# A hybrid attention block on one core: the attention's product with the values as fp32 matmuls of one query block, the mask inside the scan, and one 32-wide inverse by a transpose

## The chip, the cores and the metric

The kernel runs on one core of a Trainium2 chip. A core has five engines that run their own instruction queues side by side: PE (TensorE, matrix products, with its weight loads shown as a row of their own, PEld), DVE (VectorE), ACT (ScalarE), POOL (GpSimd) and SP (SyncE, which here only issues DMAs). The metric is the device time of one execution in microseconds (us). The kernel before takes 717.94 us (median of three runs, 717.68 to 718.83).

## The reference

The input is 1024 tokens of 1024 channels. After an RMS norm, one projection gives the inputs of two groups of heads that work side by side: eight heads of stick-breaking attention (64 channels each) and four heads of a gated DeltaNet (128 channels each). Both outputs are normed and gated, then one output projection, the residual and a last norm follow. What the change touches is the attention, and one step in the DeltaNet's triangular inverse:

```
z    = q_block @ k[:end].T / sqrt(64)            # one block of 128 queries, keys 0 .. end
causal = s < t
tail = sum over s < j < t of softplus(z[t, j])
attn = where(causal, exp(log_sigmoid(z) - tail), 0)
o    = attn @ v[:end]
```

The weight of key s for query t is thus sigmoid(z[t, s]) times the product of 1 - sigmoid(z[t, j]) over the keys j between s and t. Everything is float32.

## The kernel before, in words

All arithmetic is written through helper recorders, so nearly every instruction has the line 315 (the call in `Recorder`); instructions are told apart by the names of their tiles. The order of the work is set by a planner inside the kernel (`Model`, `Stream`, `interleave`). Each part of the program is a generator (`attention`, `window`, `delta_solve`, `delta_scan`, `projections` and so on) that emits instructions and yields a condition or a result to wait for. The planner keeps a clock of its own with a cost for every instruction (`cost`, and in `pull` a least distance between the starts of two matmuls), takes the ready generator of the lowest priority number, and so fixes the order on each engine before anything runs. The projections have the number 100 and fill PE where no attention (10) and no DeltaNet (0 to 0.7) is ready. On the chip each engine then works through its list in that order.

Stages. First the query projections, then the values and the keys of the first heads, then a long middle in which attention, DeltaNet and the remaining projections are interleaved, and last the output projection. A product in "high and low" form splits a float32 operand into a part rounded to fp32r (a float32 format whose matmul shows as one record in the trace) and the rest, and adds the products (`mm3` uses three; the names end in h and l).

Attention runs over eight heads, and in each over four windows of two query blocks (`window`, `w` from 0 to 3; a token for each window, and at most three at once). For each block of 128 queries:

- PE makes z in a PSUM bank (`pz`) from `q2` and the keys in high and low form, `kh` and `kl`. On the last 128 keys, the diagonal block, a third matmul (`maskr` by `ident`) adds -1e30 where the key isn't before the query.
- ACT writes sigmoid(z) to `sg` and sigmoid(-z) back to the bank. DVE runs a scan from the last key to the first (`cc`, the running product). POOL multiplies `sg` by `cc` shifted by one key: the attention weights, queries on partitions, keys along the row.
- PE transposes them 128 by 128 (`ident`, `sg`) into `pz`, up to four blocks at a time. ACT copies these to `ah` (fp32r) and DVE puts the rest into `al`.
- PE multiplies with the values. The stationary operand is `v2a`, 128 keys by 128 columns: 64 of the values' high part and 64 of their low part (`v2e`, written by `v_evac` with one ACT and one DVE instruction). The moving operand is `ah`, then `al`, for both query blocks at once (256 columns). The sum is in the one bank `po`, values on partitions.
- ACT copies it to `o`, PE transposes it back (`ident`, `o`), DVE adds the high and the low half (`oe`), SP stores it.

In the DeltaNet's inverse (`gdn_inv`), 32 by 32 blocks are inverted from 16 by 16 ones. Both the inverse (`xc`) and its transpose (`wc`) are updated by 16 small matmuls each (`xc`, `yt` and `yt`, `xc`), and DVE adds both results.

Of the kernel before, what the change touches and what calls it, by code (L numbers as in the profile page):

```python
# [29 lines left out]
WINDOWS = 3  # L30
# [107 lines left out]
class Model:  # L138
# [141 lines left out]
    def pull(self):  # L280
        if self.pe and not self.pe_busy and not self.pe[0].waits:
# [3 lines left out]
            at = max(self.now, op.ready, self.pe_began + 0.834 * op.columns)  # L285
# [137 lines left out]
def block(tc, xT_d, x_d, n1_d, wE_d, wQ_d, wC_d, conv_d, alog_d, dtb_d, mixw_d, wo_d, fnw_d, out_d):  # L423
# [4 lines left out]
    with ExitStack() as top:  # L428
# [34 lines left out]
        maskr = cst.tile([P, P], F32R, name="maskr")  # L463
        rbc = cst.tile([P, T], F32, name="rbc")
        make_identity(nc, rbc[:, 0:P])
        A.activation(identr, rbc[:, 0:P], AF.Copy)
# [5 lines left out]
        v_s = dr.tile([NB, P, SBH, 2, SBD], F32R, name="v_s")  # L472
# [57 lines left out]
        for tag, bufs in (("kh", 1), ("kl", 1), ("q2", 1), ("v2a", 2), ("v2a", 2), ("cc", 2), ("cc", 2), ("sg3", 1)):  # L530
            chl.append(at_.tile([P, 2, 520], F32R, tag=tag, bufs=bufs, name="chl"))
        sm = at_.tile([P, 768], F32, tag="sg2", name="sm")
# [63 lines left out]
        def diagonal(g):  # L596
            dg = at_.tile([P, 2, P], F32, tag="o2", bufs=2, name="dg")
# [18 lines left out]

        G.affine_select(zero, zero, pattern=[[-1, P]], compare_op=ALU.is_gt, fill=-1e30, base=0, channel_multiplier=1)
        A.activation(maskr, zero, AF.Copy)
# [12 lines left out]
        busy = {"w0": 0, "w1": 0, "w2": 0, "w3": 0, "T": 0, "al": 0, "po": 0, "inv": 0}  # L631
# [3 lines left out]
        def values(part):  # L635
            cs = slice(264 * part, 264 + 256 * part)
            n = 264 - 8 * part
            for b in range(NB):
                if part == 0 and 4 < b < 7:
                    row_scale(b - 5, dgs)  # L640
                if part == 0 and 4 <= b < 6:
                    dgs = [diagonal(2 * (b - 4) + g) for g in range(2)]
# [16 lines left out]
        def decays(me):  # L659
# [35 lines left out]
            cs = at_.tile([P, 2 * P], F32, tag="al", bufs=2, name="cs")  # L695
# [247 lines left out]
        def gdn_inv(h, g):  # L943
# [39 lines left out]
            xv = x0p[:, 0:2 * P].rearrange("p (u c i) -> p u c i", u=2, c=4)  # L983
# [121 lines left out]
        def attention():  # L1105
            yield lambda: "sp" in flags
            for i in range(2):
                ccs.append(at_.tile([P, T + 1], F32, tag="cc", bufs=2, name="cc"))
                V.memset(ccs[i][:, T:T + 1], 1.0)
            for h in range(SBH):  # L1110
                yield lambda: f"k{h // 2}" in flags
                kh = at_.tile([P, T], F32R, tag="kh", name="kh")
                kl = at_.tile([P, T], F32R, tag="kl", name="kl")
                q2 = at_.tile([P, T], F32R, tag="q2", name="q2")
                v2 = at_.tile([P, NB, P], F32R, tag="v2a", bufs=2, name="v2a")
# [6 lines left out]
                S.dma_start(v2.bitcast(F32), v_s[:, :, h].rearrange("b s u d -> s b (u d)").bitcast(F32))  # L1122
                hd[h] = (q2, kh, kl, v2)
# [288 lines left out]
```

## Time and profile before

| what | value |
|---|---|
| median of 3 runs | 717.94 us |
| the profiled execution | 717.07 us, its span 715.3 us |
| PE busy | 692.1 us, 97% of the span |
| DVE busy | 554.8 us, 78% |
| ACT busy | 364.6 us, 51% |
| POOL busy | 262.1 us, 37% |
| mean granted PE clock | 0.989 |
| DMA, share of 16 engines | 41% |

The span runs from the first to the last instruction; 1.8 us of the execution lie around it. Matmuls overlap one another, and each is drawn with a modelled end, so PE's busy time overstates what it does: what a matmul takes of PE is read from the distance between two starts. A float32 matmul that isn't in fp32r shows as two records, with two weight loads. In a row of a timeline, the first number is the start and the second the length, both in us, then engine, line, operation and tiles, `x` how many were merged into the row, and in brackets how long the engine had been idle and what ended it.

### The profile page before, as it was taken

How to read it: one execution, taken by the hardware profiler on the slowest of the kernel's cores; microseconds unless marked ns; L12 is line 12 of the kernel's file. 1: busy time of each engine (PE TensorE's matmuls, PEld its weight loads, DVE VectorE, ACT ScalarE, POOL GpSimd, SP SyncE). 2: the span in 40 equal slices, each digit the busy share in tenths (PEclk: the TensorE clock that was granted, in tenths of full speed). 3: DMA queues.
4: the chain of work that ended last, by engine and by line, in shares of the span. 5: the costliest groups of instructions: out<-in, count | busy, mean ns of one | idle time of the engine just before them, and what ended most of it. 6: DMA issues, size and time to landing. Idle time of an engine off the chain costs nothing.

```text
span 715.3 us, 13641 instructions
## 1 busy us (share of the span) xinstructions
PE 692.1 (97%) x4830; PEld 585.8 (82%) x4830; DVE 554.8 (78%) x1463; ACT 364.6 (51%) x887; POOL 262.1 (37%) x224
## 2 busy tenths in 40 slices
PE   8999999999899999999999899999999999899995
PEld 7889998888778888778888789888879888678885
DVE  5463616669899998968899778989788887898843
ACT  5661247437657542435667446866467852421212
POOL 0000157535434324232443244554244474443221
PEclk9999999999999999999999899999999999999998
DMA  8945374280512042226225027341615275646321
GB/s 313 359 144 213 118 269 148 71 254 7 177 38 61 24 122 65 63 75 211 60 65 155 29 78 214 101 157 45 192 58 168 61 228 191 226 163 211 100 100 59
DMA packets 76500, 96.45 MB, mean 135 GB/s; under 512 B 24656, under 2 KB 45712, under 8 KB 76432
## 3 DMA queue, kind: packets, MB, share of 16 engines
q1 hardware_dynamic: 76432, 95.58, 41.1%
q8 instruction: 38, 0.62, 0.4%
q14 instruction: 30, 0.25, 0.1%
HBM read 67.67 MB, written 27.89 MB: 134 GB/s over the span
## 4 chain that ended last, share of the span: by engine, by line
PE 78%; DVE 16%; issue 3%; ACT 2%; POOL 1%; POOLq 0%; DVEq 0%
PE pp L315 49%; PE pz L315 21%; PE po L315 6%; PE pc L315 3%; DVE cc L315 2%; DVE tm L315 2%; DVE pp L315 2%; DVE al L315 1%; DVE ac L315 1%; DVE xs L315 1%; DVE w L315 1%; DVE y L315 1%; DVE xinv L315 1%; DVE pre L315 1%; DVE wol L315 1%
## 5 line engine op out<-in xcount | busy, mean ns | idle before, releaser
L315 PE MATMUL pp<-xh,weh 128*128 128x512 f32 x384 | 162.4, 423 | 0.4 <-DVE ac L315 0.2
L315 PE MATMUL pp<-xh,wel 128*128 128x512 f32 x384 | 151.5, 394 | 0.0
L315 PE MATMUL pp<-xl,weh 128*128 128x512 f32 x384 | 150.9, 393 | 0.0
L315 POOL TENSOR_TENSOR sg<-sg,cc 128x128 f32<-128x128 f32 (+3 forms) x64 | 77.0, 1206 | 104.2 <-DVE cc L315 51.2
L315 POOL TENSOR_TENSOR wel<-wer,weh 128x512 fp32r<-128x512 f32 x48 | 61.9, 1292 | 97.8 <-ACT weh L315 86.7
L315 PEld LDWEIGHTS pp<-xh,wel 128*128 128x128 f32 x384 | 72.5, 189 | 16.2
L315 PEld LDWEIGHTS pp<-xh,weh 128*128 128x128 f32 x384 | 72.9, 190 | 12.0 <-issue 0.9
L315 PEld LDWEIGHTS pp<-xl,weh 128*128 128x128 f32 x384 | 73.0, 190 | 9.7
L315 ACT ACTIVATE sg<-pz,rs 128x384 f32<-128x384 f32 (+3 forms) x96 | 54.0, 588 | 23.7 <-PE pz L315 22.9
L315 ACT ACTIVATE ah<-pz 128x512 fp32r<-128x512 f32 (+1 forms) x80 | 43.5, 560 | 33.9 <-PE pz L315 33.2
L315 DVE TENSOR_TENSOR_SCAN cc<-pz,one 128x384 f32<-128x384 f32 (+2 forms) x64 | 54.0, 848 | 3.5 <-ACT pz L315 3.1
L315 DVE TENSOR_TENSOR al<-pz,ah 128x512 fp32r<-128x512 f32 (+1 forms) x80 | 49.9, 630 | 6.5 <-ACT ah L315 5.9
L315 PE MATMUL pp<-wol,mh 128*128 128x512 f32 (+1 forms) x136 | 52.0, 383 | 1.1 <-DVE wol L315 1.1
L315 PE MATMUL pp<-woh,mh 128*128 128x512 f32 (+1 forms) x136 | 52.4, 385 | 0.0
L315 ACT ACTIVATE pz<-pz,ns 128x384 f32<-128x384 f32 (+3 forms) x96 | 52.1, 566 | 0.0
L315 PE MATMUL pp<-woh,ml 128*128 128x512 f32 (+1 forms) x136 | 51.8, 381 | 0.0
L315 DVE TENSOR_TENSOR tm<-xs,br 128x8 f32<-128x8 f32 (+14 forms) x120 | 49.9, 416 | 0.8
L315 PE MATMUL pp<-chl,xh 128*128 128x264 f32 (+1 forms) x256 | 46.8, 284 | 0.0
L315 PE MATMUL pz<-ident,sg 128*128 128x128 f32 x288 | 43.7, 277 | 3.0 <-DVE cc L315 1.4
L315 PE MATMUL po<-ah,v2a 128*128 128x256 f32 (+1 forms) x160 | 43.5, 295 | 0.0
L315 DVE SCALAR_TENSOR_TENSOR pp<-pre,conv,pp 128x512 f32<-128x512 f32 x48 | 36.1, 752 | 7.8 <-ACT pp L315 7.5
L315 DVE TENSOR_TENSOR_SCAN cc<-pz,cc,one 128x512 f32<-128x512 f32 (+1 forms) x32 | 38.7, 1210 | 1.9 <-ACT pz L315 1.5
(240 smaller groups left out, 1649.6 us busy)
## 6 DMA issues: line engine op xcount, KB each, us to landing
wer<-wE SPq DMA_DIRECT2D x48, 256.0 KB, 3.8
xr<-x SPq DMA_DIRECT2D x16, 512.0 KB, 6.5
qk_s<-xq SPq DMA_DIRECT2D x8, 512.0 KB, 5.1
v_s<-v2e SPq DMA_DIRECT2D x16, 256.0 KB, 2.0
q<-qk_s SPq DMA_DIRECT2D x8, 512.0 KB, 4.5
v2a<-v_s SPq DMA_DIRECT2D x8, 512.0 KB, 7.3
kh<-qk_s SPq DMA_DIRECT2D x8, 512.0 KB, 4.0
kl<-qk_s SPq DMA_DIRECT2D x8, 512.0 KB, 6.0
```

The source lines that it names most:

```text
L315: ins = f(*args, **kw).ins
```

## The change

The product with the values. The attention weights are transposed as before, but ACT copies them into one float32 tile `at`, and nothing is split. `at` is now the stationary operand, 128 keys by 128 queries, and the values are the moving one, 64 columns of plain float32 (`va`). The result has queries on partitions, so it is copied by ACT (`oe`) and stored as it is: the transpose back, the copy `o` and the DVE sum are gone. The values are written by one ACT copy each (`ve`), at half the size. Work goes by single query blocks: eight windows for a head, a token for each, at most six at once.

The mask. The -1e30 matmul is gone. A tile `step` holds 384 columns of zeros and then the identity; the scan reads it backwards on the diagonal block, starts from 0, and takes max(z' * state, step) in place of a product: on the diagonal the state becomes 1, and nothing before it counts. Elsewhere it takes the maximum with 0.

The 32-wide inverse. The transpose `wc` is updated by its 16 matmuls, and `xc` is made from it by a DVE transpose; the other 16 matmuls and one DVE addition are gone.

The planner's least distance between two matmul starts goes by the type of the stationary operand's matmul (0.42 ns a column for fp32r, 0.834 for float32), and a few tiles have other buffers. The kernel's numbers (`WINDOWS`) and tile tags aside, this is the diff:

```diff
-WINDOWS = 3
+WINDOWS = 6
...
-            op.columns = int(np.prod(inputs[0].shape[1:]))
+            op.load = int(np.prod(inputs[0].shape[1:])) * (0.42 if inputs[0].dtype == F32R else 0.834)
...
-            at = max(self.now, op.ready, self.pe_began + 0.834 * op.columns)
+            at = max(self.now, op.ready, self.pe_began + op.load)
...
-        identr = cst.tile([P, P], F32R, name="ident")
-        ident = identr.bitcast(F32)
-        one = cst.tile([P, 1], F32, name="one")
-        V.memset(one, 1.0)
+        step = cst.tile([P, 512], F32, name="step")
+        ident = step[:, 384:512]
...
-            v2 = at_.tile([P, 4, 2, SBD], F32R, tag=("al", "ah")[b % 2], bufs=2, name="v2e")
-            A.activation(v2[:, :, 0, :], src, AF.Copy, scale=rstd[:, b:b + 1])
-            V.scalar_tensor_tensor(v2[:, :, 1, :], src, rstd[:, b:b + 1], v2[:, :, 0, :].bitcast(F32), ALU.mult, ALU.subtract)
-            S.dma_start(v_s[b, :, h0:h0 + 4, :, :].bitcast(F32), v2.bitcast(F32))
+            ve = at_.tile([P, 4, SBD], F32, tag="at", bufs=3, name="ve")
+            A.activation(ve, src, AF.Copy, scale=rstd[:, b:b + 1])
+            S.dma_start(v_s[b, :, h0:h0 + 4, :], ve)
...
-                    TE.matmul(xv[quads[q], 1, c, :], xc[quads[q], c, :], yt[quads[q], c, :], start=True, stop=True)
-            for q in range(4):
-                if q == 0:
-                    yield
-                for c in range(4):
-                    TE.matmul(xv[quads[q], 0, c, :], yt[quads[q], c, :], xc[quads[q], c, :], start=True, stop=True)
-            r = [V.tensor_tensor(wc, xv[:, 1], wc, ALU.add), V.tensor_tensor(xc, xv[:, 0], xc, ALU.add)]
+                    TE.matmul(xv[quads[q], c, :], xc[quads[q], c, :], yt[quads[q], c, :], start=True, stop=True)
+            V.tensor_tensor(wc, xv, wc, ALU.add)
+            r = V.transpose(xc.rearrange("p c i -> p (c i)"), wc.rearrange("p c i -> p (c i)"))
...
-                    if s1 == end:
-                        TE.matmul(z[:, n - P:n], identr, maskr, start=False, stop=False)
...
-                    V.tensor_tensor_scan(cc[:, s0:s1][:, ::-1], z[:, 0:n][:, ::-1], one.to_broadcast([P, n]),
-                                         1.0 if s1 == end else cc[:, s1:s1 + 1], ALU.mult, ALU.mult)
+                own = step[:, 512 - n:512][:, ::-1] if s1 == end else step[:, 0:1].to_broadcast([P, n])
+                V.tensor_tensor_scan(cc[:, s0:s1][:, ::-1], z[:, 0:n][:, ::-1], own,
+                                     0.0 if s1 == end else cc[:, s1:s1 + 1], ALU.mult, ALU.max)
...
-                    ah = at_.tile([P, 512], F32R, tag="ah", bufs=2, name="ah")
-                    al = at_.tile([P, 512], F32R, tag="al", bufs=2, name="al")
-                    A.activation(ah[:, 0:n * P], tp[:, 0:n * P], AF.Copy)
-                    r = V.tensor_tensor(al[:, 0:n * P], tp[:, 0:n * P], ah[:, 0:n * P].bitcast(F32), ALU.subtract)
+                    at = at_.tile([P, 512], F32, tag="at", bufs=3, name="at")
+                    r = A.activation(at[:, 0:n * P], tp[:, 0:n * P], AF.Copy)
...
-                    for m, t in enumerate((ah, al)):
-                        TE.matmul(ov[:, i0 * P:256], v2[:, s, :], t[:, c], start=(s == 0 and m == 0), stop=(s == 2 * w + 1 and m == 1))
+                for u in range(n):
+                    k = 4 * (j - 1) + u
+                    TE.matmul(ov, at[:, u * P:(u + 1) * P], va[:, k, :], start=k == 0, stop=k == b)
...
-            o2 = at_.tile([P, 256], F32, tag="o2", bufs=2, name="o2")
-            yield A.activation(o2, ov[:, 0:256], AF.Copy)
+            oe = at_.tile([P, SBD], F32, tag="oe", bufs=4, name="oe")
+            yield A.activation(oe, ov, AF.Copy)
             busy["po"] = 0
-            op = pz()
-            for i in range(2):
-                TE.transpose(op[:, i * P:(i + 1) * P], o2[:, i * P:(i + 1) * P], ident)
-            oe = at_.tile([P, 2, SBD], F32, tag="oe", bufs=2, name="oe")
-            V.tensor_reduce(oe, op[:, 0:256].rearrange("p (i u d) -> p i d u", i=2, u=2), AX.X, ALU.add)
-            flags[f"e{h}{w}"] = S.dma_start(o_s[2 * w:2 * w + 2, :, h * SBD:(h + 1) * SBD].rearrange("b t d -> t b d"), oe)
+            flags[f"e{h}{b}"] = S.dma_start(o_s[b, :, h * SBD:(h + 1) * SBD], oe)
```

How the order moves, at two places. On PE, in the last window of the first head, before the change (`o` and `sg` are transposed, `ident` is the identity; numbers behind a name tell one buffer from another):

```order
L315 MATMUL po<-ah,v2a 128x256
L315 MATMUL po<-al,v2a 128x256
L315 MATMUL po<-ah,v2a 128x128
L315 MATMUL po<-al,v2a 128x128
L315 MATMUL pz<-kh,q_1537 128x512
L315 MATMUL pz<-maskr,ident 128x128
L315 MATMUL pz<-kl,q_1537 128x512
L315 MATMUL pz<-kh,q_1537 128x512
L315 MATMUL pz<-kl,q_1537 128x512
L315 MATMUL pz<-ident,o_2046 128x128 x2
L315 MATMUL pz<-ident,sg 128x128 x8
```

On PE at the same place after the change, from the first head's query block 5 to 7 (`step` now holds the identity):

```order
L315 MATMUL pz<-kh,q_1512 128x512
L315 MATMUL pz<-kl,q_1512 128x512
L315 MATMUL po<-va,at 128x64 x6
L315 MATMUL pz<-step,sg 128x128 x7
L315 MATMUL po<-va,at 128x64 x7
L315 MATMUL pp<-xh,weh 128x512
L315 MATMUL pp<-xl,weh 128x512
L315 MATMUL pp<-xh,wel 128x512
```

The mask matmuls and the transposes of `o` are gone, and a block's products stand together, as many as it has key blocks, where groups of `ah` and `al` stood; the transposes of `sg` and the pairs of `kh` and `kl` stay. Between two groups of products there are other matmuls, but at one place here only the next transposes.

On DVE at that place before the change (`tm` and `xs` are the DeltaNet's 16-wide inverse, `pre` a projection's result, the `cc` rows are the scans):

```order
L315 TENSOR_TENSOR al<-pz,ah 128x512
L315 TENSOR_TENSOR tm<-xs,br 128x64
L315 TENSOR_TENSOR al<-pz,ah 128x512
L315 TENSOR_REDUCE xs<-tm 128x4
L315 SCALAR_TENSOR_TENSOR cc<-pz,one 128x512
L315 TENSOR_TENSOR al<-pz,ah 128x384
L315 SCALAR_TENSOR_TENSOR cc<-pz,cc,one 128x512
L315 COPY pre<-pre 128x3
L315 TENSOR_TENSOR pre<-pp,rbc 128x512
L315 TENSOR_REDUCE oe<-pz 128x128
```

And on DVE after the change, between the scans of the first head's last blocks:

```order
L315 SCALAR_TENSOR_TENSOR cc<-pz,step 128x384
L315 TENSOR_TENSOR tm<-xs,br 128x4x11
L315 SCALAR_TENSOR_TENSOR cc<-pz,cc,step 128x512
L315 TENSOR_REDUCE xs<-tm 128x4
L315 MEMSET pre 128x3
L315 TENSOR_TENSOR pre<-pp,rbc 128x512
L315 TENSOR_TENSOR tm<-xs,br 128x4x12
L315 SCALAR_TENSOR_TENSOR pp<-pre,conv,pp 128x512
```

Of the attention only the scans are left on DVE; `al` and `oe` no longer stand between them and the rest.

More of the change, by code (lines that the diff above doesn't have):

```diff
@@ L462, in block @@
         ns8 = cst.tile([P, NB], F32, name="ns8")
-        maskr = cst.tile([P, P], F32R, name="maskr")
         rbc = cst.tile([P, T], F32, name="rbc")
-        make_identity(nc, rbc[:, 0:P])
-        A.activation(identr, rbc[:, 0:P], AF.Copy)
+        make_identity(nc, ident)
+        V.memset(step[:, 0:384], 0.0)
         rsg = cst.tile([P, GH, NB], F32, name="rsg")
@@ L471, in block @@
         qk_s = dr.tile([8, 2, P, T], F32R, name="qk_s")
[L472 removed]
+        v_s = dr.tile([NB, P, SBH, SBD], F32, name="v_s")
         gate_s = dr.tile([NK, P, T], F32, name="gate_s")
@@ L630, in block @@
         gst = {}
-        busy = {"w0": 0, "w1": 0, "w2": 0, "w3": 0, "T": 0, "al": 0, "po": 0, "inv": 0}
+        busy = {**{f"w{b}": 0 for b in range(NB)}, "T": 0, "al": 0, "po": 0, "inv": 0}
         def values(part):
@@ L641, in values @@
                 if part == 0 and 4 <= b < 6:
-                    dgs = [diagonal(2 * (b - 4) + g) for g in range(2)]
+                    dgp = at_.tile([P, 2, 256], F32, tag="sg3", name="dg")
+                    dgs = [diagonal(dgp, 2 * (b - 4) + g) for g in range(2)]
                 yield lambda: ps.room("pp", 2)
@@ L1121, in attention @@
                     loads.append(S.dma_start(t.bitcast(F32), src.bitcast(F32)))
-                S.dma_start(v2.bitcast(F32), v_s[:, :, h].rearrange("b s u d -> s b (u d)").bitcast(F32))
-                hd[h] = (q2, kh, kl, v2)
+                S.dma_start(va, v_s[:, :, h].rearrange("b s d -> s b d"))
+                hd[h] = (q2, kh, kl, va)
                 yield loads
-                for w in range(4):
-                    tok = f"w{w}"
+                for b in range(NB):
+                    tok = f"w{b}"
@@ L1163, in window @@
             parts = []
[L1164 to L1166 removed]
+            last = b // 4
+            for j in range(last + 2):
+                if j <= last:
+                    yield lambda: busy["al"] < 3
                     busy["al"] += 1
[L1168 to L1169 removed]
+                    n = min(4, b + 1 - 4 * j)
                     tp = pz()
[L1171 to L1177 removed]
+                    for u in range(n):
+                        TE.transpose(tp[:, u * P:(u + 1) * P], sg[:, (4 * j + u) * P:(4 * j + u + 1) * P], ident)
+                    at = at_.tile([P, 512], F32, tag="at", bufs=3, name="at")
+                    r = A.activation(at[:, 0:n * P], tp[:, 0:n * P], AF.Copy)
+                    if j == last:
                         busy["T"] = 0
                         busy[tok] = 0
[L1180 removed]
+                    parts.append((at, n, r))
                     yield
```

93 lines of the change are left out of this document (37 added, 56 removed).

## The prediction

> **What bounds the kernel now.** I read the page first (busy shares, the chain that ended last), then the busy time by stages, then PE's waits.
>
> ```profile
> PE 692.1 (97%) x4830; PEld 585.8 (82%) x4830; DVE 554.8 (78%) x1463; ACT 364.6 (51%) x887; POOL 262.1 (37%) x224
> PE 78%; DVE 16%; issue 3%; ACT 2%; POOL 1%; POOLq 0%; DVEq 0%
> 60.00:150.00 90.00, 90.00 (x560) 81.42 (x559) 45.32 (x114) 39.49 (x84) 38.69 (x40) 1.00 0.47 160
> 150.00:590.00 440.00, 428.94 (x3441) 361.32 (x3440) 387.26 (x1040) 263.40 (x703) 181.29 (x145) 0.99 0.35 105
> 590.00:705.00 115.00, 112.56 (x529) 91.48 (x528) 89.44 (x242) 26.58 (x42) 39.05 (x30) 1.00 0.47 159
> ```
>
> The last three rows give, for a stretch of the span, its length and then the busy time of PE, PEld, DVE, ACT and POOL, the granted clock, the DMA share and GB/s. The attention lies wholly in the stretch from 150 to 590 us. PE is idle there for 440 - 428.94 = 11.1 us, and a clock of 0.99 loses another 440 x 0.01 = 4.4 us: 15.5 us is all that PE could win there without doing less. DVE is nearly as full, 387.3 of 440 us (88%), and the chain runs through it for 16% of the span. So the kernel is PE's work in a fixed order, with small stalls where DVE is late:
>
> ```profile
> PE po L315 <- ACT ident L315: 2.5, 1, 2.5
> PE pz L315 <- DVE al L315: 2.1, 2, 1.2
> PE pz L315 <- DVE cc L315: 1.4, 1, 1.4
> PE pz L315 <- DVE w L315: 1.3, 1, 1.3
> PE pz L315 <- DVE oe L315: 0.9, 1, 0.9
> 184.00:188.00 4.00, 4.00 (x16) 3.52 (x17) 2.86 (x5) 1.04 (x3) 2.16 (x2) 0.57 1.03 333
> 405.00:413.00 8.00, 7.61 (x33) 6.69 (x34) 4.62 (x14) 3.48 (x7) 1.31 (x1) 0.58 0.03 7
> ```
>
> The waits (total, times, longest) are nearly all on DVE, apart from the one for the identity at the start, and the change deletes `al` and `oe`. The clock's loss sits in two places, with 0.57 and 0.58 granted, each behind a stall.
>
> **The change, PE's side.** What a matmul costs when PE is full is the distance between starts. For the new product, float32 with 128 by 128 weights and only 64 moving columns, the nearest row is another float32 matmul with such weights and 32 moving columns (`sm`, two matmuls, four records). Weight loads:
>
> ```profile
> 86.75 0.53 PEld L315 LDWEIGHTS pz<-sm 128*128 128x128 f32 x4
> 87.20 0.30 PEld L315 LDWEIGHTS pp<-chl,xh 128*128 128x128 f32 x2
> ...
> 208.42 0.54 PEld L315 LDWEIGHTS pz<-w,dt 64*64 64x64 f32 x8 [0.71 <-issue]
> ...
> 536.24 0.19 PEld L315 LDWEIGHTS po<-ah,v2a 128*128 128x128 f32 x1
> ...
> 537.18 0.30 PEld L315 LDWEIGHTS pc<-state,kq 128*128 128x128 f32 x2
> ```
>
> Four loads take 87.20 - 86.75 = 0.45 us, 0.1125 each, with almost nothing to stream: the load sets the pace. Weights of 64 columns go faster (eight loads within 0.54 us, under 0.07 each), so it is the 128 columns that cost. A product matmul is two records, 0.225 us, and there are 36 key blocks x 8 heads = 288 of them: 64.8 us. Before, the eight loads from 536.24 to 537.18 are one group of `ah` and `al`, 0.94 / 8 = 0.1175 each; 320 of them make 37.6 us. The product costs PE 27.2 us more.
>
> The Trainium skill ("TensorE: Matmul & The Clock Gate", section on the back-to-back issue gap) has about 81 ns for a load and matmul pair in a stream with 128 columns. By it the 576 records would take an estimated 46.7 us, and the product would cost 9.1 us more instead of 27.2. The measured 112.5 ns stands against it here, so it is only a rival below. The same page (section on weight-path modes) says that fast weight load is on for 128 weights whose type isn't FP32, which speaks against this change; but the fp32r loads above are no closer together (117.5 ns) than the float32 ones, so the sum doesn't take it.
>
> What goes from PE:
>
> ```profile
> 611.71 0.39 PE L315 MATMUL pp<-woh,ml 128*128 128x512 f32 x1
> 611.94 1.47 PE L315 MATMUL pz<-ident,mx 128*128 128x128 f32 x12
> ...
> 613.48 0.39 PE L315 MATMUL pp<-wol,mh 128*128 128x512 f32 x1
> ...
> 200.99 0.80 PE L315 MATMUL pz<-yt,xc 32*32 32x32 f32 x29
> ...
> 202.42 0.39 PE L315 MATMUL po<-ah,v2a 128*128 128x256 f32 x1
> ...
> 537.69 0.22 PE L315 MATMUL pz<-maskr,ident 128*128 128x128 f32 x1
> ...
> 537.75 0.40 PE L315 MATMUL pz<-kl,q 128*128 128x384 f32 x1
> ```
>
> The mask is bounded from below by the last two rows, 0.06 us to the start of `kl`, and from above by one load, 0.1125, because the loads for `kl` have to follow: 64 masks are 3.8 to 7.2 us; I take 6.0, nearer the load, since every row above is paced by loads. Transposes: twelve of them and one 512-column matmul (0.23 us, 611.94 - 611.71) lie between 611.94 and 613.48, so one is 0.109 us, and the 64 of `o` are 7.0 us. The inverse's step: 64 records from 200.99 to 202.42, 0.0223 each; half of them go in each of eight units, 256 in all, 5.7 us. PE's sum is 27.2 - 6.0 - 7.0 - 5.7 = +8.5 us. All of it lies in the full stretch, so without shorter stalls all of it shows.
>
> **The change, the other engines.**
>
> ```profile
> L315 DVE TENSOR_TENSOR al<-pz,ah 128x512 fp32r<-128x512 f32 (+1 forms) x80 | 49.9, 630 | 6.5 <-ACT ah L315 5.9
> L315 DVE TENSOR_REDUCE oe<-pz 128x128 f32<-128x256 f32 x32 | 13.3, 416 | 3.5 <-PE pz L315 3.3
> L315 DVE TENSOR_TENSOR xc<-pz,xc 128x128 f32<-128x128 f32 x8 | 2.2, 278 | 0.0
> L315 DVE STREAM_TRANSPOSE wc<-xc 128x128 f32<-128x128 f32 x8 | 2.4, 300 | 0.0
> L315 DVE TENSOR_TENSOR_SCAN cc<-pz,one 128x512 f32<-128x512 f32 x16 | 19.4, 1215 | 0.1
> L315 DVE TENSOR_TENSOR_SCAN cc<-pz,cc,one 128x512 f32<-128x512 f32 x24 | 30.6, 1277 | 1.0 <-ACT pz L315 0.7
> L315 ACT ACTIVATE ah<-pz 128x512 fp32r<-128x512 f32 x48 | 28.3, 606 | 15.9 <-PE pz L315 15.4
> L315 ACT ACTIVATE ah<-pz 128x384 fp32r<-128x384 f32 x32 | 15.8, 492 | 17.9 <-PE pz L315 17.8
> L315 ACT ACTIVATE o<-po 128x256 f32<-128x256 f32 x32 | 12.4, 386 | 13.8 <-PE po L315 13.6
> L315 ACT ACTIVATE goe<-pz 128x128 f32<-128x128 f32 x32 | 8.9, 279 | 12.3 <-PE pz L315 12.2
> L315 ACT ACTIVATE wqh<-wq 128x256 fp32r<-128x256 f32 x2 | 0.8, 408 | 1.9 <-DMA wq<-wQ 1.9
> v_s<-v2e SPq DMA_DIRECT2D x16, 256.0 KB, 2.0
> v2a<-v_s SPq DMA_DIRECT2D x8, 512.0 KB, 7.3
> ```
>
> DVE loses `al` and `oe`, 49.9 + 13.3 = 63.2 us, all in the stretch: 387.3 becomes 324.1 of 440, 74% instead of 88%. (The halved `v2e` work comes before 150 us, where PE has no idle time, and gives nothing.) The addition to `xc` becomes a transpose, 278 to 300 ns eight times, nothing. The scans keep count and shapes; no row shows one with a maximum and a table as second operand, so 0 is my value, the two forms above being 62 ns apart, with 96 x 0.062 = 6 us of DVE time as the bound on either side, below DVE's slack.
>
> ACT copies 96 tiles `at` instead of 80 `ah`: with 606, 492, 386 and 279 ns for four, three, two and one block, 48 x 0.606 + 16 x (0.492 + 0.386 + 0.279) = 47.6 us against 28.3 + 15.8 = 44.1. The 64 copies `oe` are below 64 x 0.279 = 17.9 us against 12.4. Together +9.0: 263.4 becomes 272.4 of 440, 62%, under a PE that is full; no cost as long as ACT has that slack. Behind a late ACT copy stand the sigmoids of the next block, for which the scans wait, and PE's next products.
>
> DMAs: the values' stores and loads are halved. The stores of `o` become 64 of half the size instead of 32; the DMA share is 0.35 in the stretch and nothing reads them before the end. The head's tiles `kh` and `q2` have two buffers, so loads come earlier. No cost. The identity no longer passes through ACT, for which PE waited 2.5 us at the start; the gain is between 0 and 2.5 us, and I take 0, because the first real product needs `wqh`, which waits for its DMA.
>
> **The stalls.** This is the term I have to choose. Deleting `al` and `oe` takes 2.1 + 0.9 us at once. DVE's free time in the stretch goes from 52.7 to 115.9 us, and each product group holds PE longer than before, during which scans and copies catch up. If the waits fell as DVE's load relative to its free time does, from 387 / 53 = 7.3 to 324 / 116 = 2.8, they would be 0.38 of 15.5, 5.9 us. I go a little below that, 3.5 us, because the two places with half a clock need a stall of some length ahead of them to happen at all. The stalls give back 12.0 us; the ends for the range are 0 and 15.5.
>
> The sum against the profiled execution: 717.07 + 8.5 - 12.0 = 713.6 us. The median of the runs, 717.94, lies 0.87 above that execution, so 714.4 us.
>
> **Rivals.**
>
> ```profile
> 239.99 1.30 DVE L315 TENSOR_TENSOR t0u<-t0u,sso 128x4 f32<-128x4 f32 x1
> 288.41 1.22 DVE L315 TENSOR_TENSOR tm<-xs,br 128x48 f32<-128x48 f32 x1
> 537.44 0.38 ACT L315 ACTIVATE o<-po 128x256 f32<-128x256 f32 x1
> ```
>
> *The stalls stay: slower.* PE also waits behind DVE instructions of the DeltaNet that take far longer than their four or 48 columns would, 1.30 and 1.22 us in these rows, shortly ahead of waits of the inverse; the change leaves them alone. If the stalls come from such single late links and not from DVE's load, only the `al` and `oe` waits go: 717.94 + 8.5 - 3.0 = 723.4 us. It decides as soon as less than 7.1 us are given back. For it: PE's work is certain to grow, the gain is not. Against it: the deletion takes a sixth of DVE's work in the stretch.
>
> *The output bank.* 64 instead of 32 groups go through the one bank `po`, each after ACT has emptied it (537.44 is such a copy, 0.38 us). If ACT is late by 0.2 us each time, 12.8 us come on top of 714.4: 727.2. Against it: the order leaves other matmuls between most groups.
>
> *Shorter loads.* If the product's records went at the pace of the 64-column weights, 0.54 / 8 = 0.0675 us, they would take 38.9 us, and PE would win 17.4 us instead of paying 8.5: 700.5 us without any gain from stalls, 688.5 with 12 of it. Against it stand the `sm` loads, which are the same kind of load. By the skill's 81 ns (same page and section) it would be 696 to 708 us.
>
> **How the numbers follow.** A run's spread is about 0.2%, 1.4 us; closer than that I call the same. Chances: my forecast 50%, with its own range 711 to 718.5 (8 to 15 us given back), four fifths of that faster; the stalls stay 30%, 720 to 727; the bank 6%, 725 to 735; shorter loads 8%, 688 to 706 for paces nearer 0.0675 than 0.1125; the rest 6%, mixtures of both signs. Faster by more than 0.2%: 40 + 8 + 2 = 50%; within it 10 + 2 + 1 = 13%; slower 28 + 6 + 3 = 37%. The range 704 to 727 leaves out most of the shorter loads and the upper part of the bank.
>
> **What the profile after would show.** The `va` records start 0.11 us apart and 64.8 us in all (0.07 to 0.08 would prove the shorter loads). DVE's busy time falls to about 484 us, ACT's rises to about 374. PE's idle time from 150 us to the end of the attention falls from 11 to about 3 us, and the clock is 0.99 or more throughout. If that idle time stays near 10 us, or PE waits for ACT's `oe` or `at`, I am wrong on the stalls, and the kernel is slower.

## The result and the profile after

The changed kernel takes 719.31 us (median of 20 runs, 717.08 to 722.36), against 718.07 us for the kernel before in the same runs (20 runs, 717.53 to 719.82). The ratio is 1.0015, with a 95% interval of 1.0002 to 1.0027: 0.15% slower, where 3.5 us less were forecast. The time lies inside the forecast range, 704 to 727 us, but on the other side of no change. The profiled execution took 719.67 us, its span 717.9 us, at a mean clock of 0.992. The ratios, here and below, leave out executions that took over 1.5% longer than the fastest of their kernel, and the medians keep them.

The lines of the changed kernel's page that answer to those of before are the busy shares, the shares of the chain that ended last, and the busiest new groups:

```profile
PE 696.9 (97%) x4702; PEld 593.3 (83%) x4702; DVE 497.0 (69%) x1335; ACT 363.6 (51%) x931; POOL 260.4 (36%) x223
PE 88%; DVE 5%; ACT 3%; issue 2%; POOL 1%; DMA 1%; SPq 0%; POOLq 0%; DVEq 0%; ACTq 0%
```
```profile
L315 PEld LDWEIGHTS po<-va,at 128*128 128x128 f32 x576 | 73.5, 192 | 6.5 <-ACT at L315 2.2 <-ACT oe L315 0.2
L315 DVE TENSOR_TENSOR_SCAN cc<-pz,step 128x512 f32<-128x512 f32 x16 | 19.4, 1212 | 2.2 <-ACT pz L315 2.2
L315 ACT ACTIVATE oe<-po 128x64 f32<-128x64 f32 x64 | 14.6, 228 | 35.1 <-PE po L315 34.4
```

The chain of waits now runs through PE for 88% of the span (78% before) and through DVE for 5% (16% before), so DVE was relieved as intended. The table of the middle stretch (length, then busy time of PE, PEld, DVE, ACT, POOL, clock, DMA share, GB/s) shows what that was worth:

```profile
150.00:590.00 440.00, 429.42 (x3299) 365.85 (x3298) 333.51 (x921) 265.88 (x755) 177.77 (x145) 0.99 0.34 102
```

DVE is down from 387.3 to 333.5 us, yet PE is still idle for 440 - 429.42 = 10.6 us, against 11.1 before and the 3 us that the prediction named as its mark. PE's waits (total, times, longest) have moved, not gone:

```profile
PE pz L315 <- DVE xs L315: 3.6, 2, 2.5
PE po L315 <- POOL step masks.py:199: 1.4, 1, 1.4
PE pp L315 <- DVE ac L315: 1.3, 2, 0.9
PE pp L315 <- DVE wol L315: 1.1, 2, 0.9
PE po L315 <- ACT at L315: 1.0, 2, 0.6
```

The waits for `al`, `oe`, `cc` and `w` are gone from PE's waits, and the one for `xs`, 0.3 us before, is now the largest. It sits where one head's last block is done and the next head begins. First PE's timeline there, then DVE's, then two rows of SP, which issues the DMAs:

```profile
363.47 1.78 PE L315 MATMUL po<-va,at 128*128 128x64 f32 x14 [0.36 <-ACT at L315]
365.06 0.30 PE L315 MATMUL pz<-kh,q 128*128 128x128 f32 x1
...
370.16 1.09 PE L315 MATMUL pz<-step,sg 128*128 128x128 f32 x4 [2.51 <-DVE xs L315]
371.93 1.12 PE L315 MATMUL pz<-step,sg 128*128 128x128 f32 x4 [0.69 <-ACT at L315]
372.70 0.78 PE L315 MATMUL pp<-xh,weh 128*128 128x512 f32 x1
373.28 0.63 PE L315 MATMUL pp<-xl,weh 128*128 128x512 f32 x1
373.70 0.63 PE L315 MATMUL pp<-xh,wel 128*128 128x512 f32 x1
```
```profile
366.67 0.42 DVE L315 TENSOR_TENSOR_SCAN cc<-pz,step 128x128 f32<-128x128 f32 x1 [3.17 <-ACT pz L315]
...
369.32 0.69 DVE L315 TENSOR_TENSOR_SCAN cc<-pz,step 128x256 f32<-128x256 f32 x1 [0.52 <-DMA br<-bd]
369.34 0.07 DVE L315 MEMSET br<- 128x16 f32 x1
369.93 0.17 DVE L315 COPY xs<-x 128x64 f32<-128x64 f32 x1
```
```profile
358.17 7.69 SPq L315 DMA_DIRECT2D o_s<-oe  x2
365.95 1.18 SPq L315 DMA_DIRECT2D br<-bd  x2
```

Several blocks of the new head start at once, ACT has two sigmoids for each, DVE stands idle for 3.17 us until the first is there, and then the next scan starts only when the DMA for `br` has landed; the scan doesn't read that tile, but a memset of it, part of the inverse, stands beside it in DVE's queue. That DMA is late for a reason of its own. DVE's last reading of the earlier `br` ended at 360.3 us, and by these rows the load could have gone then, but in SP's list it stands behind the store of the old head's last `oe`. That store waits for PE's last products and ACT's copy (365.29 us), goes out at 365.54, and the load follows at 365.95 and lands at 369.2. PE waits 2.51 us, and behind the waits the 512-column matmuls start 0.42 us apart instead of 0.23. From 350 to 400 us PE is idle for 4.9 us, nearly half of its idle time in the middle stretch, and the clock is 0.93. DVE isn't short of time here; it waits itself.

The first two rows of PE also give the price of the product: 14 records from 363.47 to 365.06 us, 0.1136 us each.

### The profile page after: what moved, and what is told of

It is laid out like the page before. It is cut to its first block, busy times and chain, and to the rows that moved or that the text cites. A ratio compares the mean times of both kernels' runs of the same rounds, so it can differ in the third digit from the quotient of the medians.

```text
span 717.9 us, 13363 instructions
## 1 busy us (share of the span) xinstructions
PE 696.9 (97%) x4702; PEld 593.3 (83%) x4702; DVE 497.0 (69%) x1335; ACT 363.6 (51%) x931; POOL 260.4 (36%) x223
## 4 chain that ended last, share of the span: by engine, by line
PE 88%; DVE 5%; ACT 3%; issue 2%; POOL 1%; DMA 1%; SPq 0%; POOLq 0%; DVEq 0%; ACTq 0%
PE pp L315 54%; PE pz L315 22%; PE po L315 9%; PE pc L315 3%; DVE cc L315 1%; DVE tm L315 1%; DVE wol L315 0%; ACT nkv L315 0%; DMA n<-n 0%; DVE pp L315 0%; ACT pz L315 0%; DVE ac L315 0%; DMA br<-bd 0%; ACT at L315 0%; ACT sg L315 0%
## 5 line engine op out<-in xcount | busy, mean ns | idle before, releaser
L315 PEld LDWEIGHTS po<-va,at 128*128 128x128 f32 x576 | 73.5, 192 | 6.5 <-ACT at L315 2.2
L315 PE MATMUL po<-va,at 128*128 128x64 f32 x576 | 74.3, 271 | 1.0 <-ACT at L315 1.0
L315 DVE TENSOR_TENSOR_SCAN cc<-pz,step 128x384 f32<-128x384 f32 (+2 forms) x64 | 53.8, 850 | 22.6 <-ACT pz L315 21.5
L315 ACT ACTIVATE at<-pz 128x512 f32<-128x512 f32 (+2 forms) x96 | 45.6, 496 | 18.4 <-PE pz L315 17.5
L315 PE MATMUL pz<-step,sg 128*128 128x128 f32 x288 | 46.0, 280 | 4.9 <-DVE xs L315 3.6
L315 DVE TENSOR_TENSOR tm<-xs,br 128x8 f32<-128x8 f32 (+14 forms) x120 | 42.7, 356 | 1.1
L315 DVE TENSOR_TENSOR_SCAN cc<-pz,cc,step 128x512 f32<-128x512 f32 (+1 forms) x32 | 38.8, 1212 | 6.6 <-ACT pz L315 5.7
```

The costliest lines, as they stand in the source:

```text
L315: ins = f(*args, **kw).ins
```

## The experiments

Times of one group of runs are compared with runs of the kernel before on the same chip, whose medians were 716.7 to 717.6 us. A held order means that the planner counts the instructions of the original kernel, so that each engine works through the same list but for the rows that the edit names.

### The changed kernel again, and a longer warm-up

> The changed kernel again, unchanged, for the others of this group to be compared with: 717 to 722 us. In its first profile PE stood idle for 4.9 us between 350 and 400 us, behind one late DVE chain, and the clock was 0.93 there. If that place is a property of the order, it is in this profile too (4 to 6 us idle, 0.93 or less); if it is a chance of single runs, it is absent here and the run is near 717.

```diff
         for _ in range(8):
             TE.matmul(qp[7][:, 0:P], ident, ident, start=True, stop=True)
+        for _ in range(4):
+            nc.tensor.matmul(qp[7][:, 0:P], ident, ident, start=True, stop=True)
```

> Twelve warm-up matmuls in place of eight, the order of everything else held. Theory: with the identity no longer through ACT the warm-up starts 1 us earlier, ends before the first product can start, and the clock is halved for the first products; then four more matmuls close the gap and the kernel gains 1.5 to 2 us. Rival: the start is late because the first loads land later; then nothing changes (0 to 0.3 us), or 0.5 us are lost.

The changed kernel again: 719.26 us, ratio 1.0014 (1.0000 to 1.0029). Its profile has the same place with the same wait, so that is a property of the order:

```profile
367.94 1.09 PE L315 MATMUL pz<-step,sg 128*128 128x128 f32 x4 [2.55 <-DVE xs L315]
```

Its instructions lie 2.2 us earlier than in the first profile, from 20 to 370 us. The reason is the clock at the start. These rows are the first products, in the first profile and in the second:

```profile
1.43 3.78 PE L315 MATMUL po<-step 128*128 128x128 f32 x16 [1.43 <-POOL step masks.py:199]
5.76 0.80 PE L315 MATMUL pp<-xh,wqh 128*128 128x512 f32 x1 [0.55 <-ACT xh L315]
...
9.27 0.63 PE L315 MATMUL pz<-xl,wqh 128*128 128x512 f32 x1
9.70 0.63 PE L315 MATMUL pz<-xh,wql 128*128 128x512 f32 x1
```
```profile
1.43 3.58 PE L315 MATMUL po<-step 128*128 128x128 f32 x16 [1.43 <-POOL step masks.py:199]
5.42 0.49 PE L315 MATMUL pp<-xh,wqh 128*128 128x512 f32 x1 [0.41 <-ACT xh L315]
...
8.17 0.40 PE L315 MATMUL pz<-xh,wqh 128*128 128x512 f32 x1
8.40 0.40 PE L315 MATMUL pz<-xl,wqh 128*128 128x512 f32 x1
```

In the first, matmuls still start 0.43 us apart at 9.7 us, in the second 0.23. The warm-up starts 1.0 us earlier than before (1.43 instead of 2.46), ends 0.41 to 0.55 us ahead of the first product, and whether the clock is full by then differs from execution to execution: ten or eleven of the first products ran at half speed in three of seven profiles of kernels with this warm-up, at most one in the other four, and none to five in the twelve profiles with the identity through ACT. The Trainium skill ("TensorE: Matmul & The Clock Gate", section on the clock gate and the warm-up) says that the full clock comes after a busy window of about 3.4 us that runs freely; a warm-up of 3.8 us with a gap behind it would then do or not do by where it falls in the window. The two profiles agree with that, though neither shows the window itself. With twelve warm-up matmuls the start was full in the one profile taken, and the median 717.99 us, ratio 1.0023 (1.0000 to 1.0046): the gain of 1.5 to 2 us isn't established.

### The parts, each with the order that the planner finds

The inverse's step alone, the mask alone and both, on the kernel before; and the product alone, which is the changed kernel with those two undone.

```diff
-                    TE.matmul(xv[quads[q], 0, c, :], yt[quads[q], c, :], xc[quads[q], c, :], start=True, stop=True)
...
+            r = V.transpose(xc.rearrange("p c i -> p (c i)"), wc.rearrange("p c i -> p (c i)"))
```

> The kernel before with the inverse's step by a transpose, and nothing else. By the prediction's term 5.7 us faster, if PE is full there. Rival: the 16 small matmuls of a unit ran inside a chain of waits and only the planner's order moves: between 2 us faster and 2 us slower.

```diff
-                    if s1 == end:
-                        TE.matmul(z[:, n - P:n], identr, maskr, start=False, stop=False)
...
+                    own = step[:, 512 - n:512][:, ::-1] if s1 == end else step[:, 0:1].to_broadcast([P, n])
```

> The kernel before with the mask in the scan, and nothing else of the change (two small tiles share a buffer to make room for the table, and the identity still passes through ACT). By the prediction's term 6.0 us faster, 3.8 to 7.2 by its bounds. Rival: DVE's waits set the middle, and then less than 2 us.

Both edits in one kernel:

> Both of these together on the kernel before, with its old product. If the terms add, 11.7 us faster, about 706 us, which beats both kernels. Rival: with less work on PE the stalls behind DVE grow, as DVE's load is unchanged: 5 us faster or less.

The new product, with `maskr` and the two sets of 16 matmuls as they were:

```diff
+                if s1 == end:
+                    TE.matmul(z[:, n - P:n], identr, maskr, start=False, stop=False)
...
+                    TE.matmul(xv[quads[q], 0, c, :], yt[quads[q], c, :], xc[quads[q], c, :], start=True, stop=True)
```

> The changed kernel with the mask and the inverse's step as they were before, and the identity through ACT again: the new product alone. PE's work grows by 27.2 - 7.0 = 20.2 us. With the 12 us of stalls that the prediction gave back, 8 us slower than before; with the 7 us that the profiles show, 13 us slower; with none, 20.

| kernel | median us | ratio to before (95%) |
|---|---|---|
| inverse's step alone | 716.18 | 1.0000 (0.9978 to 1.0021) |
| mask alone | 718.28 | 1.0035 (1.0013 to 1.0057) |
| both | 701.95 | 0.9815 (0.9794 to 0.9837) |
| product alone | 725.48 | 1.0089 (1.0056 to 1.0122) |

Only the product alone did about what the terms say (8 us slower expected with the 12 us of stalls, 6 to 9 measured). Each small part gains nothing, and both together gain more than their sum. Parts that don't add up like this point to something that is in no term: every edit makes the planner find another order.

### One nanosecond in the planner

```diff
-            return n * 0.445 + 1
+            return n * 0.445 + 2
```

The planner's cost of an fp32r matmul, which touches no instruction. On the kernel before, on the changed kernel, and on the kernel before with mask and inverse changed; the last row takes a nanosecond away instead (`n * 0.445`).

> The kernel before with the same instructions, the planner counting one nanosecond more for each fp32r matmul: another order, no other work. If the order alone moves the time by as much as one of the change's terms, it lands 3 to 10 us away from before, on either side. If not, within 1.5 us, and the missing gains of the single parts need another cause.

> The changed kernel with the same one nanosecond: again only another order. By the first theory 3 to 10 us away from the changed kernel's 719.3, by the second within 1.5 us of it.

> The kernel before with the mask in the scan and the inverse's step by a transpose (701.95 us with its own order), the planner counting one nanosecond more for each fp32r matmul: the same instructions in another order. If the 14.7 us were mostly luck of that order, it lands nearer to the 716 us of the run with the held order: 706 to 716 us. If they belong to the work that is gone, 700 to 705 us.

> The changed kernel, the planner counting one nanosecond less for each fp32r matmul: a third order of the same instructions (719.3 and 716.6 us for the first two). If orders differ by as much as the runs so far say, 712 to 726 us, and it is as likely to be faster than before as slower.

| kernel | its own order, us | one nanosecond away, us | ratio to before (95%) |
|---|---|---|---|
| before | 717.5 | 724.99 | 1.0105 (1.0072 to 1.0138) |
| mask and inverse on before | 701.95 | 721.28 | 1.0063 (1.0033 to 1.0093) |
| changed | 719.3 | 716.61 | 1.0002 (0.9982 to 1.0022) |
| changed, less 1 ns | 719.3 | 727.44 | 1.0078 (1.0044 to 1.0113) |

(By its ratio the last row stands for some 723 us.) The same instructions in another order take 7.5 us more for the kernel before, 18 to 19 us more for the one that looked best, 1 to 3 us less or 4 us more for the changed one. So the 14.7 us belonged to one order and not to the work. The 701.95 us are real, and that kernel is the one version with all of the arithmetic that clearly beats both, but its edits don't explain why. The chain of that kernel, first in its lucky order and then one nanosecond away, differs:

```profile
PE 86%; DVE 9%; issue 2%; ACT 2%; DMA 0%; POOLq 0%; POOL 0%; DVEq 0%
```
```profile
PE 77%; DVE 15%; ACT 4%; issue 3%; DMA 1%; POOLq 0%; POOL 0%; SPq 0%; DVEq 0%; ACTq 0%
```

The instructions are the same, 4510 matmul records each; the spans are 700.2 and 716.9 us. The chain runs through DVE for 15% instead of 9%, and the mean clock was 0.987 instead of 0.995, which makes an estimated 6 of the 17 us (0.008 of 717).

### The single terms, with the order held

The stalls alone: DVE's `al` left out, PE's work unchanged. (With `instead`, the planner counts the instruction that is written, and the chip gets another, or with `None` none.)

```diff
-                    r = V.tensor_tensor(al[:, 0:n * P], tp[:, 0:n * P], ah[:, 0:n * P].bitcast(F32), ALU.subtract)
+                    r = V.tensor_tensor(al[:, 0:n * P], tp[:, 0:n * P], ah[:, 0:n * P].bitcast(F32), ALU.subtract, instead=None)
...
-                        TE.matmul(ov[:, i0 * P:256], v2[:, s, :], t[:, c], start=(s == 0 and m == 0), stop=(s == 2 * w + 1 and m == 1))
+                        TE.matmul(ov[:, i0 * P:256], v2[:, s, :], t[:, c], start=(s == 0 and m == 0), stop=(s == 2 * w + 1 and m == 1),
+                                  instead=lambda o, v, a, **k: nc.tensor.matmul(o, v, ah[:, c], **k))
```

> The kernel before without DVE's 80 subtractions `al`; the products that read `al` read `ah` instead, so PE's work is the same and the low part is left out of the result. The order is held. This is the prediction's term for the stalls alone. If DVE's load makes the stalls, 8 to 13 us faster (12.0 in the prediction, 15 between the kernel before and the new product alone). If they come from single late links or from the order, under 4 us.

It takes 711.49 us, ratio 0.9924 (0.9897 to 0.9951): 5.5 us faster, 3.5 to 7.4 by the interval, between the 8 to 13 us expected if DVE's load makes the stalls and the under 4 us if single late links do. The page's shares and the middle stretch:

```profile
PE 690.4 (97%) x4830; PEld 584.6 (82%) x4830; DVE 514.1 (72%) x1383; ACT 364.7 (51%) x887; POOL 262.1 (37%) x224
```
```profile
150.00:590.00 440.00, 432.62 (x3465) 364.89 (x3464) 352.94 (x974) 265.15 (x706) 182.71 (x147) 0.99 0.35 108
```

DVE has 34 us less to do in the stretch, and PE's idle time there falls from 11.1 to 7.4 us only.

The other way round, on the changed kernel: DVE gets the subtractions back, into the bank that it reads, and nothing on PE waits for their result.

```diff
                     r = A.activation(at[:, 0:n * P], tp[:, 0:n * P], AF.Copy)
+                    late.append((r, nc.vector.tensor_tensor(tp[:, 0:n * P], tp[:, 0:n * P], at[:, 0:n * P], ALU.subtract)))
```

> DVE gets back the 96 subtractions that `al` cost it (into the same bank, 50 us of DVE time; the product does not wait for them), the order of everything else held. If DVE's load is what made PE's stalls, as the prediction had it, what was given back goes again: 7 us slower by the stalls that the two profiles show, 12 us by the prediction. If the stalls are single late links, 0 to 2 us slower.

738.16 us, ratio 1.0280 (1.0258 to 1.0302): 19 us slower than the changed kernel, more than either theory gave. It isn't the price of DVE's load alone: the bank is held longer, too, and the mean clock of the profiled execution is 0.976 instead of 0.992, an estimated 12 of the 21 us between the two profiled executions.

PE's freed time on the kernel before: the inverse's step, the mask, both, and both with `al` left out as well.

```diff
-                    TE.matmul(xv[quads[q], 0, c, :], yt[quads[q], c, :], xc[quads[q], c, :], start=True, stop=True)
+                    TE.matmul(xv[quads[q], 0, c, :], yt[quads[q], c, :], xc[quads[q], c, :], start=True, stop=True, instead=None)
...
-                        TE.matmul(z[:, n - P:n], identr, maskr, start=False, stop=False)
+                        TE.matmul(z[:, n - P:n], identr, maskr, start=False, stop=False, instead=None)
```

> The kernel before with the 16 matmuls and the transpose in place of 32 matmuls, but every other instruction in the order that it had: the planner still counts the matmuls that are gone. If the term of 5.7 us is right where it stands and it was the new order that ate it in the run without a held order (no gain there), 4 to 6 us faster. If the matmuls were covered by waits of the inverse, under 2 us.

> The kernel before without the 64 mask matmuls (the mask is left out, not moved into the scan), the order held in the same way. If PE's term is right, 4 to 6 us faster, against 1.6 us slower with the free order and the mask in the scan. If PE's freed time becomes waits for DVE at once, under 2 us.

> The kernel before without the mask matmuls (the mask is left out) and with the inverse's step by a transpose, the order held. By the prediction 11.7 us faster. By the two single runs with a held order, where the freed PE time became waits, about 3 us; then the 14.7 us that both gave with a free order came mostly from the new order.

> The two runs before in one: no `al` on DVE, no mask matmuls, 16 matmuls fewer in each inverse, the order held. If PE's freed time turned into waits because DVE was the bound in those stretches, it must count once DVE is relieved: 10 to 12 us faster than the run without `al` alone, 20 to 24 us faster than before. If PE's time in those places is covered by the chains themselves, 3 to 5 us beyond the run without `al`.

| left out, order held | median us | ratio to before (95%) | expected by PE's terms |
|---|---|---|---|
| 16 matmuls in each inverse | 718.38 | 1.0007 (0.9985 to 1.0028) | -5.7 us |
| mask matmuls | 714.35 | 0.9979 (0.9958 to 1.0000) | -6.0 us |
| both | 715.96 | 0.9978 (0.9959 to 0.9996) | -11.7 us |
| both and `al` | 706.37 | 0.9869 (0.9843 to 0.9895) | -11.7 us beyond -5.5 |

On the kernel before, 11.7 us of PE's work are worth 1.6 us (0.3 to 2.9 by the interval), and 4 us more than `al` alone (0.9869 against 0.9924) once DVE is relieved. The expectation had 10 to 12 us there if DVE's load was the bound, and 3 to 5 us if the chains of waits themselves cover PE's time. So DVE's load explains the smaller part, and which waits take the rest isn't shown. At one place the held order lets one see how freed time is lost, instruction by instruction. The wait that grows there is in the list of the kernel before, where the prediction passed over it:

```profile
PE pz L315 <- DVE xinv L315: 1.5, 4, 0.5
```

PE's timeline around an inverse, in the kernel before and then without the 16 matmuls:

```profile
198.69 0.89 PE L315 MATMUL pz<-wc,dt 16*32 16x32 f32 x32
...
204.79 0.39 PE L315 MATMUL pp<-xh,weh 128*128 128x512 f32 x1
...
208.45 0.65 PE L315 MATMUL pz<-w,dt 64*64 64x64 f32 x8 [0.31 <-DVE xinv L315]
...
212.50 0.49 PE L315 MATMUL pc<-nkv,xinv 128*128 128x128 f32 x2 [0.65 <-DVE xinv L315]
```
```profile
198.57 0.89 PE L315 MATMUL pz<-wc,dt 16*32 16x32 f32 x32
...
204.05 0.39 PE L315 MATMUL pp<-xh,weh 128*128 128x512 f32 x1
...
208.22 0.65 PE L315 MATMUL pz<-w,dt 64*64 64x64 f32 x8 [0.65 <-DVE xinv L315]
...
212.35 0.49 PE L315 MATMUL pc<-nkv,xinv 128*128 128x128 f32 x2 [0.72 <-DVE xinv L315]
```

Ahead of the inverse, at 198 us, the second profile is 0.12 us early. At 204 us it is 0.74 us early: the 16 matmuls gave PE 0.62 us, near the predicted 0.71 for one inverse. Four microseconds later PE waits 0.65 us for DVE's `xinv` where it waited 0.31, and by 212 us it is 0.15 us early, nearly what it was at first. DVE had hardly a pause to shorten, as the stretch of the kernel before shows (third busy time):

```profile
200.00:220.00 20.00, 19.04 (x217) 15.70 (x216) 18.64 (x63) 13.71 (x45) 4.97 (x4) 1.00 0.15 41
```

Last, the same PE work put back into the changed kernel, without effect on the result (`zr` holds zeros):

```diff
+                if s1 == end:
+                    nc.tensor.matmul(z[:, n - P:n], zr, zr, start=False, stop=False)
...
+                    nc.tensor.matmul(xu[quads[q], c, :], yt[quads[q], c, :], xc[quads[q], c, :], start=True, stop=True)
```

> The changed kernel with 64 matmuls of 128 columns on the diagonal blocks (of zeros) and 16 more matmuls in each inverse, both without effect on the result: PE's work of the mask and of the old inverse again, the order held. By the prediction 11.7 us slower than the changed kernel. If half of PE's time is covered by waits there, about 6 us.

728.14 us, ratio 1.0173 (1.0139 to 1.0206): 9 us more than the changed kernel by the medians, 11 by the ratios (1.0173 against 1.0015), of the 11.7 counted. Its chain runs through PE for 90% of the span and through DVE for 4%.

And PE's new work itself, cut in half:

```diff
-                    at = at_.tile([P, 512], F32, tag="at", bufs=3, name="at")
+                    at = at_.tile([P, 512], F32R, tag="at", bufs=3, name="at")
```

(and `ve` and `va` likewise)

> The product as one fp32r record instead of two float32 ones; the low part of values and weights is left out. The order of everything is held. If PE is full and each record costs a load, 288 x 0.1125 = 32.4 us go, less what then shows as waits: 25 to 32 us faster. If the records cost less than a load (0.08 us), 23 us at most. If other engines set the middle, under 15 us.

696.90 us, ratio 0.9697 (0.9675 to 0.9719): 22.4 us faster than the changed kernel, of 32.4 counted. That is somewhat below the 25 to 32 us of the first theory, and close to the 23 us of shorter records. But its records are no shorter: seven of its weight loads lie between 354.36 and 355.13 us, 0.11 us each. So 32 us of PE's work went, and the rest shows as waits and clock: PE's idle time from 150 to 590 us is 14.0 us instead of 10.6, and the mean clock 0.982 instead of 0.992.

## Why the prediction was wrong

The step that failed is "the stalls give back 12.0 us". The prediction scaled all of PE's waits with DVE's ratio of busy to free time. Measured on the kernel before, with PE's work unchanged and the order held, taking `al` from DVE gives back 5.5 us; in the changed kernel PE's idle time in the stretch is 10.6 us where 3 were forecast. With 5.5 in place of 12.0 the prediction's own sum is 717.94 + 8.5 - 5.5 = 720.9 us; 719.3 were measured. That it comes so close is in part luck, since the order alone moves the changed kernel by up to 4 us. Its rival "the stalls stay" said that less than 7.1 us decides for slower, and named single late links as the cause. The profile shows late links, though not the slow DVE instructions of the DeltaNet that the rival named: the place at 364 to 372 us waits on ACT, on a DMA and on the order of DVE's and SP's queues. The rival's own 723.4 us were too high by 4, because the waits shrank by more than `al` and `oe` alone.

- *The product: right.* 0.1125 us for a record were forecast, 0.1136 stand in the trace, and the run with one record fewer for each product has 0.11 us too. The shorter loads did not come, nor the 81 ns that the Trainium skill gives ("TensorE: Matmul & The Clock Gate", section on the back-to-back issue gap).
- *Mask and inverse, -11.7 us in full: near on the changed kernel, where that work put back cost 9 to 11 us, and wrong on the kernel before, where it is worth 1.6.* That the sentence "so without shorter stalls all of it shows" nearly held because the new product had made PE the bound (chain 88%) is argued and not shown. On the kernel before, PE at 97% busy was not the bound everywhere: at the inverse shown PE waits for a DVE that is full, and with DVE relieved of `al` the same work is still worth only 4 us.
- *The DMAs, "no cost": wrong at one place.* Nothing reads the stores of `oe` before the end, as the prediction says, but one of them held up the load of `br` behind it in SP's list, and the chain that ended last runs through that load. What this costs, no run shows.
- *The clock's "stall of some length": not always.* The second profile of the changed kernel has a spell of half clock inside a stretch in which PE is busy throughout (last section).
- *The identity, 0 within 0 to 2.5 us of gain: the bound was one-sided.* No gain came, and some starts lost 2 us to the half clock; an effect on the clock was not thought of.
- *The output bank: right to leave out.* PE waits 1.0 us in all for `at` at `po`, another 0.7 for it at `pz`, and appears nowhere waiting for `oe`.
- *Busy times.* DVE fell to 497.0 us, not 484: the durations of DVE's instructions add up to 73 us less, but they overlap one another, and the busy time falls by 58. The scans cost nothing more, as forecast (1212 ns in the first form, 1215 before). ACT stayed at 363.6 instead of 374; one `oe` took 228 ns, not the bound of 279.
- *Not in the sum at all: the order.* The prediction counted moved instructions as free. One nanosecond in the planner moves the kernel before by 7.5 us and the changed one by -1 to -3 or +4. A forecast of -3.5 us lies within that, so by this spread its chances for faster and slower should have been nearly even.

What stays open: which property of an order makes it 10 us better. The chain's DVE share isn't it: it is 16% in both orders of the kernel before, and in the changed one 5% in its own order and 8% in the faster one. The mean clock goes with the time in all three pairs of profiled executions (0.995 and 0.987, 0.989 and 0.981, 0.994 and 0.992, the faster first), but it makes only part of the difference, and no run changed it alone. Loading `br` ahead of the store of `oe`, moving its memset off DVE's queue, or starting fewer blocks at a head's change, wasn't tried. The product alone ran only with an order of its own. Its 6 to 9 us, against 20.2 us of added PE work, would speak for 11 to 14 us given back, near the predicted 12 and not the 5.5 of the held order; they mix new work with a new order, and no run here takes them apart.

## What to carry to other kernels

The waits here belonged to places in the order more than to an engine's load: to price a relief, go through the waits one by one and ask what is late next, rather than scaling their sum. That goes for the queue that issues the DMAs, too: a store that waits for its data holds up the loads behind it. Where two engines are nearly full (here 97% and 88% of the stretch), taking work from one of them gave only a part of its size. The same work added to the changed kernel cost nearly all of its size, or more; how much of this lies in adding instead of taking away and how much in the other kernel isn't separated here. And where a planner makes the order, try a meaningless change of its costs first: its spread is the least difference that an edit must make before its own terms can be believed.

## What the runs showed of the hardware

- The clock can be at half speed while the granted clock reads 1.00: in the first 10 us of the changed kernel's first profile 512-column matmuls start 0.43 us apart, and the clock's column (third from the end) says 1.00. Only the distances show it.

```profile
0.00:10.00 10.00, 8.03 (x25) 6.56 (x26) 3.13 (x7) 4.90 (x7) 0.70 (x6) 1.00 0.69 227
```

- Two executions of one program agree to 0.05 us over hundreds of microseconds and differ by a few steps of 2 to 3 us: the 2.2 us at the start, and a spell of half clock between 410 and 421 us that only the second profile of the changed kernel has. It cost 3.2 us, so that the second ended 0.8 us later although its products had started 2.2 us earlier. PE was busy throughout (the number behind the length below), its last waits before were of 0.19 and 0.32 us, and the first profile has the same waits (0.19 and 0.33 us) without the spell. Most of the spread of the 20 runs, 717.1 to 722.4 us, has the size of such steps.

```profile
410.00:420.00 10.00, 10.00 (x76) 8.28 (x76) 6.21 (x38) 2.08 (x9) 0.00 (x0) 0.71 0.07 18
```
